# A retention layer in two phases: all projections by seven products first, then the recurrence

## The chip, the cores and the metric

The kernel runs on one core of a Trainium2 chip. The metric is the device time of one execution in microseconds; three runs of the kernel before the change are given, and one more execution was taken by the hardware profiler. In the text PE is TensorE, DVE is VectorE, ACT is ScalarE, POOL is GpSimd and SP is SyncE, whose queue carries most DMAs.

## The reference

Two layers of a hybrid decoder work on 1040 tokens (16 meta tokens and 1024 others) of width 1024, in float32. Layer 0 mixes a gated linear recurrence with windowed attention, layer 1 is a multi-scale retention; each has a SwiGLU feed-forward network behind it. The change lies in the retention:

```python
def _mixer_retention(h, cos, sin, w_in, w_out):
    q, k, v, g = jnp.split(h @ w_in, SPLIT_RET, axis=-1)      # 1024, 1024, 2048, 2048 wide
    q = _rotary(q.reshape(B, T, RET_HEADS, RET_QK_DIM), cos, sin)
    k = _rotary(k.reshape(B, T, RET_HEADS, RET_QK_DIM), cos, sin) * (RET_QK_DIM ** -0.5)
    ...
    def step(state, chunk):                                   # chunks of 128 tokens, 4 heads
        qn, kn, vn = chunk
        qk = jnp.einsum('bhid,bhjd->bhij', qn, kn).astype(F32) * decay_intra
        o = (jnp.einsum('bhij,bhjv->bhiv', qk, vf)
             + jnp.einsum('bhid,bhdv->bhiv', qn.astype(F32) * decay_q[..., None], state))
        state = (decay_chunk[:, None, None] * state
                 + jnp.einsum('bhjd,bhjv->bhdv', kn.astype(F32) * decay_k[..., None], vf))
        return state, o
    ...
    o = _rms_noaffine(o).reshape(B, T, 2 * D_MODEL).astype(h.dtype)
    return (jax.nn.silu(g) * o) @ w_out
```

`h` is the RMS-normed residual stream, and the mixer's result is added to it.

## The kernel before

**Precision and products.** Activations stand feature-major: 8 blocks of 128 features by tokens. Every large product is made of three matmuls (`mm3`, L160 to L162): both operands are split into a high part, rounded by ScalarE to the matmul's short format, and a low part, the difference (VectorE or GpSimd); the product of the two low parts is left out. `part` (L111, L113) splits weights, 512 columns at a time, `hilo` (L782, L783) splits moving blocks.

**Strassen.** The feed-forward layers (`ffn`) use a form of Strassen's scheme with seven products in place of eight. A unit is 256 inputs by 256 outputs per pair of blocks. `unit22` loads a unit of weights, makes the sums S1 to S4 on GpSimd (L145 to L151) and splits seven operands. The moving side is a 2 by 2 block matrix as well: two feature blocks by two halves of the tokens, with T1 to T4 made by `mixed` (L777). `seven` runs the products and calls `evac` after each, which adds or copies PSUM into the result. In front of a layer the T blocks are not there yet; `eight` runs its first two units as plain products.

**The order.** The program is written in one stream, and a planner places every instruction on its engine's queue, by the place in the stream and by when its inputs and its memory are free; engines run their queues in order. SBUF has 56 slots of 531 columns (`slot`), PSUM four banks under `ps` and four under `ax`.

**Layer 0's feed-forward** takes 22 tiles of hidden features, in 11 pairs. The hidden blocks go to DRAM, and the down projection takes them back in groups `DGROUPS` (two, three, three and three pairs) with four units of outputs in each. After a unit of the last group, `done0` prepares that block of the residual stream for the retention: a split of `h` times the gain (`xh`, `xl`, L963) of the first half of the tokens, its square, and the sum of the squares on GpSimd.

**Retention** goes over the tokens in two halves (16 + 512 and 512). In each half, for each of the four heads: values are projected by plain products with the tokens as the stationary operand, 256 columns of weights a time (`wrv`), the meta tokens apart in `mm_meta` (L186); keys and queries by `proj` with 264 or 512 columns and rotated (`rotate`); gates by `proj`. The recurrence over blocks of 128 tokens has `first` (scores L1083, transposed keys L1098), `second` (outputs, state update L1127, split of the state by `to_hilo` L294 and L295) and `third` (transposes L1137, gate, split). Gates and the next head's keys are placed between the blocks (`fill`), then `project` adds the output projection into `h` (L1208). All of the projection weights are thus loaded and split once for each half. The norm factor comes from `stats`, once per half, and is applied behind each projection. For the last head of a half, `prefetch` and `project` also prepare the next stage, for the second half the normed blocks of layer 1's feed-forward (`normed` L762, `plain`).

## Time and profile before

| what | us |
|---|---|
| median of three runs (2689.75 to 2698.34) | 2693.39 |
| the profiled execution, its own time | 2692.1 |
| its span, first to last instruction | 2690.0 |
| to 435: input, layer 0's mixer; PE busy | 403.6 of 435 |
| 435 to 860: layer 0's gate and up; PE busy | 421.7 of 425 |
| 860 to 1093: layer 0's down; PE busy | 221.9 of 233 |
| 1093 to 2010: retention; PE busy | 909.5 of 917 |
| from 2010: layer 1's feed-forward; PE busy | 658.0 of 680 |

The stages overlap at their borders; the limits are read from the rows of the windows. In a row of a window come its limits and its length, then for PE, PE's weight loads, DVE, ACT and POOL the busy time and the number of instructions, then the granted clock of TensorE (1.00 is full speed), the busy share of the DMA engines and GB/s. In a row of a group come line, engine, operation, what it writes and reads, the shape and the count, then busy time in us and the mean in ns, then the idle time of the engine ahead of it and what ended it. In a row of the timeline come the start and the duration in us; a row of the chain of waits has the same two and names what the chain ran through.

### The profile page before, as it was taken

Reading aid. Unit: us, or ns where it says so; the run is one execution under the profiler, and the core shown is the slowest. Engines: PE = TensorE matmul, PEld = TensorE weight load, DVE = VectorE, ACT = ScalarE, POOL = GpSimd, SP = SyncE. Lnnn points to the kernel's source line nnn. Section 1 sums busy time; section 2 is a strip of 40 time slices with the busy share of each in tenths; the row PEclk is TensorE's granted clock in tenths of the full one; section 3 lists DMA queues with packets and bytes.
Section 4 is the critical chain, followed back from the end, with each engine's and each line's share of the span. In section 5 each row is a group of like instructions: output and inputs, shape, how many; then the busy total and the mean of one; then the engine's idle time right before and its main releaser. Section 6 shows DMA issues by size and latency. Waiting matters only on the chain.

```text
span 2690.0 us, 42990 instructions
## 1 busy us (share of the span) xinstructions
PE 2614.7 (97%) x16122; PEld 2328.5 (87%) x16122; DVE 1648.6 (61%) x2967; ACT 1130.2 (42%) x2328; POOL 1324.9 (49%) x1234
## 2 busy tenths in 40 slices
PE   8988999999999999999999999999998999998999
PEld 7877989999998999888889898888886788886787
DVE  7977676666666877543534444344387555556875
ACT  4666543333333434343434534334343333334442
POOL 3756233554554877523323243333353555565884
PEclk9999999999999999999999999999998999999999
DMA  4001142223225642222122242222241232226542
GB/s 153 30 26 56 55 170 69 95 103 112 84 104 171 214 141 89 91 71 79 65 85 70 86 135 71 87 79 71 86 141 62 87 114 98 101 92 236 165 151 86
DMA packets 111072, 274.62 MB, mean 102 GB/s; under 512 B 13520, under 2 KB 13776, under 8 KB 110864
## 3 DMA queue, kind: packets, MB, share of 16 engines
q1 hardware_dynamic: 87840, 228.86, 25.3%
q10 hardware_dynamic: 22464, 41.17, 4.1%
q8 instruction: 126, 2.06, 0.3%
q0 software_dynamic: 560, 1.85, 0.2%
q14 instruction: 82, 0.67, 0.1%
HBM read 216.40 MB, written 55.43 MB: 101 GB/s over the span
## 4 chain that ended last, share of the span: by engine, by line
PE 88%; DVE 6%; ACT 3%; issue 1%; POOL 1%; DMA 1%; SPq 0%; ACTq 0%; DVEq 0%; POOLq 0%
PE ps L160 20%; PE ps L161 20%; PE ps L162 20%; PE ax L160 8%; PE ax L161 8%; PE ax L162 8%; DVE lo L113 1%; PE ps L673 1%; POOL ol L783 1%; DVE ol L783 1%; PE ax L1083 1%; DVE xp L762 1%; PE ax L186 1%; DVE T L777 0%; ACT hi L111 0%
## 5 line engine op out<-in xcount | busy, mean ns | idle before, releaser
L160 PE MATMUL ps<-oh,hi 128*128 128x260 f32 (+1 forms) x1584 | 509.0, 324 | 20.0 <-ACT oh L782 11.6
L162 PE MATMUL ps<-oh,lo 128*128 128x260 f32 (+1 forms) x1584 | 508.3, 322 | 8.7 <-DVE lo L113 8.6
L161 PE MATMUL ps<-ol,hi 128*128 128x260 f32 (+1 forms) x1584 | 509.7, 322 | 1.1 <-DVE ol L783 1.1
L111 ACT CAST hi<-raw 128x512 fp32r<-128x512 f32 (+2 forms) x476 | 284.6, 602 | 520.9 <-PE ps L161 343.4
L160 PE MATMUL ax<-oh,hi 128*128 128x260 f32 (+1 forms) x1212 | 388.8, 323 | 1.7 <-ACT hi L111 0.9
L162 PE MATMUL ax<-oh,lo 128*128 128x260 f32 (+1 forms) x1212 | 387.4, 322 | 2.6 <-DVE lo L113 2.6
L161 PE MATMUL ax<-ol,hi 128*128 128x260 f32 (+1 forms) x1212 | 389.8, 322 | 0.0
L113 DVE TENSOR_TENSOR lo<-raw,hi 128x512 fp32r<-128x512 f32 (+2 forms) x348 | 286.9, 827 | 111.4 <-ACT hi L111 102.3
L160 PEld LDWEIGHTS ps<-oh,hi 128*128 128x128 f32 x1584 | 299.7, 190 | 47.5 <-ACT oh L782 14.7
L111 ACT CAST hi<-S 128x512 fp32r<-128x512 f32 (+2 forms) x288 | 161.2, 562 | 425.3 <-PE ps L161 190.7
L113 DVE TENSOR_TENSOR lo<-S,hi 128x512 fp32r<-128x512 f32 (+2 forms) x288 | 252.1, 878 | 139.5 <-ACT hi L111 136.1
L162 PEld LDWEIGHTS ps<-oh,lo 128*128 128x128 f32 x1584 | 300.3, 190 | 34.6 <-DVE lo L113 10.8
L161 PEld LDWEIGHTS ps<-ol,hi 128*128 128x128 f32 x1584 | 300.9, 190 | 25.8 <-DVE ol L783 2.1
L113 POOL TENSOR_TENSOR lo<-raw,hi 128x512 fp32r<-128x512 f32 x128 | 166.0, 1305 | 266.8 <-ACT hi L111 255.4
L160 PE MATMUL ps<-xh,hi 128*128 128x512 f32 (+1 forms) x752 | 277.2, 371 | 8.2 <-ACT hi L111 7.1
L161 PE MATMUL ps<-xl,hi 128*128 128x512 f32 (+1 forms) x752 | 274.7, 366 | 0.6 <-DVE xl L210 0.6
L162 PE MATMUL ps<-xh,lo 128*128 128x512 f32 (+1 forms) x752 | 273.1, 364 | 0.0
L291 POOL TENSOR_TENSOR t<-t,rf 128x520 f32<-128x520 f32 (+1 forms) x148 | 215.0, 1462 | 81.9 <-DVE t L824 31.7
L162 PEld LDWEIGHTS ax<-oh,lo 128*128 128x128 f32 x1212 | 229.4, 189 | 21.6 <-DVE lo L113 3.6
L160 PEld LDWEIGHTS ax<-oh,hi 128*128 128x128 f32 x1212 | 229.9, 190 | 20.8 <-ACT hi L111 1.3
L161 PEld LDWEIGHTS ax<-ol,hi 128*128 128x128 f32 x1212 | 229.9, 190 | 18.4
L783 POOL TENSOR_TENSOR ol<-raw,oh 128x520 fp32r<-128x520 f32 (+1 forms) x140 | 204.6, 1489 | 28.7 <-ACT oh L782 14.7
(325 smaller groups left out, 5720.7 us busy)
## 6 DMA issues: line engine op xcount, KB each, us to landing
raw<-in_wr_dram SPq DMA_DIRECT2D x64, 512.0 KB, 3.2
raw<-in_wgu_dram SPq DMA_DIRECT2D x48, 512.0 KB, 3.3
rb<-in_wgu_dram SPq DMA_DIRECT2D x40, 512.0 KB, 3.2
raw<-hd SPq DMA_DIRECT2D x77, 260.0 KB, 3.4
raw<-hd SPq DMA_DIRECT2D x77, 256.0 KB, 3.1
raw<-in_wrv_dram SPq DMA_DIRECT2D x32, 512.0 KB, 3.2
raw<-in_wro_dram SPq DMA_DIRECT2D x32, 512.0 KB, 3.2
hd<-T ACTq DMA_DIRECT2D x44, 260.0 KB, 2.6
```

The costliest lines, as they stand in the source:

```text
L111: nc.scalar.copy(hi, src)
L113: eng.tensor_tensor(out=lo, in0=src, in1=f32(hi), op=ALU.subtract)
L160: nc.tensor.matmul(ps, ah, bh, start=first and i == 0, stop=False, skip_group_check=more)
L161: nc.tensor.matmul(ps, ah, bl, start=False, stop=False, skip_group_check=more)
L162: nc.tensor.matmul(ps, al, bh, start=False, stop=last and i == n - 1, skip_group_check=more)
L186: nc.tensor.matmul(o, a, b, start=first and i == 0 and j == 0, stop=end and j == 1)
L291: (eng or nc.vector).tensor_tensor(out=out_, in0=a, in1=b, op=ALU.mult)
L673: nc.tensor.matmul(k.po[:n, o:o + 64], sb[:, i * P:(i + 1) * P], vt[:, k.b - len(segs) + 1 + j, g * 64:(g + 1) * 64], start=False, stop=g ...
L762: nc.vector.scalar_tensor_tensor(out=t[:, :n], in0=h[m][hf][:, :n], scalar=par(gname, m), in1=sc, op0=ALU.mult, op1=ALU.mult)
L783: eng.tensor_tensor(out=lo, in0=src, in1=f32(hi), op=ALU.subtract)
L1083: nc.tensor.matmul(ps[:, :P], kf[d][:, c:c + P], qf[d][:, c:c + P], start=d == 0, stop=d == 1)
```

## The change

The retention is taken apart into two phases.

**Phase one** makes all of the projections, for all tokens and heads, and writes them to DRAM (`kdr`, `qdr`, `gdr`, `vdr`). Its moving side `xo2` has the form of the feed-forward's: normed blocks, both halves of 520 tokens, with T blocks. Two gate units are run by `eight`, the 22 others (four of keys, four of queries, eight of values, six of gates) by `seven`. Keys, gates and values are scaled by the norm factor behind the product; keys and queries are rotated; values, which now come out feature-major, are transposed by TensorE. The weights `wr` hold all four parts in units of the Strassen form, and `wrv` goes.

**Phase two** runs the recurrence head by head over all nine blocks, reading keys, queries, values and gates back from DRAM. Beside each step stands at most one unit of the output projection of the half before (`fills`), none at steps 32 and 33. The last gate unit is placed behind the first step's loads.

**Around it.** `done0` makes normed blocks for both halves (`normed`, `spill`, `plain`) in place of the scaled splits; `late0` computes the product of the norm factors that it needs. `DGROUPS` becomes `DG`, with groups of two, three, two, two and two pairs in layer 0 and the old groups in layer 1. `eight` evacuates each product one product later. In `mixes` the low part of T3 goes to GpSimd. `ratio` can take a slot. `mm_meta` and `stats` are no longer used in the retention.

```diff
-DGROUPS = ((0, 1), (2, 3, 4), (5, 6, 7), (8, 9, 10))
+DG = (((0, 1), (2, 3, 4), (5, 6), (7, 8), (9, 10)), ((0, 1), (2, 3, 4), (5, 6, 7), (8, 9, 10)))
...
     def eight(u, xs, chunks, evac):
+        last = None
         for m, c in ((1, 1), (2, 1), (1, 2), (2, 2)):
...
-            evac(m, c, [ps[:, :b - a] for ps, (a, b) in zip(bk, chunks)])
+            if last:
+                evac(*last)
+            last = (m, c, [ps[:, :b - a] for ps, (a, b) in zip(bk, chunks)])
+        evac(*last)
...
-                    xs[j][k] = hilo(m_[k], n, new(j), nc.vector)
+                    xs[j][k] = hilo(m_[k], n, new(j), nc.gpsimd if k == "T3" else nc.vector)
...
     def done0(m):
-        spill(m, 1, 8, 512)
...
-            nc.scalar.activation(xh[:, o], src, AF.Copy, scale=g)
-            nc.vector.scalar_tensor_tensor(out=xl[:, o], in0=src, scalar=g, in1=f32(xh[:, o]), op0=ALU.mult,
-                                           op1=ALU.subtract)
...
+        for hf in range(2):
+            if m == 0:
+                acc2[hf] = slot("acc")
+            xp[m][hf] = normed(m, hf, "g2", 520, tr[hf], acc2[hf])
+            spill(m, hf, 8, 512)
+            plain(xo2, xp, m, hf, 520, slot, nc.vector)
+
+    ffn(fp, wgu0, wd0, DG[0], xo, Rf, 520, late, done0)
...
+    ALL, REST = ((0, 260), (260, 520)), ((8, 520),)
...
+        def proj7(i, chunks, fin):
+            t = {}
+            def evac(k, bk):
+                if k == 1:
+                    later()
+                key = {0: "11", 1: "11", 2: "12", 3: "22", 4: "22", 5: "12", 6: "21"}[k]
+                if k in (0, 2, 3):
+                    t[key] = slot("t")
+                    each(chunks, lambda o, ps: nc.scalar.copy(o, ps), t[key], bk)
+                    return
+                if k < 6:
+                    each(chunks, lambda o, ps, x: nc.vector.tensor_tensor(out=o, in0=ps, in1=x, op=ALU.add),
+                         t[key], bk, t[key])
+                fin(int(key[0]) - 1, int(key[1]) - 1, t.get(key), bk)
+            seven(unit22(wr[i], 512, ap), xo2, chunks, evac)
...
+        def gate(i):
+            def fin(r, c, t, bk):
+                t = scaled(REST, c, t, bk)[:, 8:520]
+                nc.scalar.activation(t, t, AF.Silu)
+                nc.scalar.dma_start(gdr[2 * i + r][c], t)
+            return fin
...
+                mul(p, a, cR)
+                mul(a, a, sR, nc.gpsimd)
+                nc.vector.tensor_tensor(out=p, in0=p, in1=r_, op=ALU.subtract)
+                nc.gpsimd.tensor_tensor(out=u, in0=u, in1=a, op=ALU.add)
+                nc.scalar.dma_start(dst[0][c], p)
+                nc.scalar.dma_start(dst[1][c], u)
...
+        first8(0, (0, 1))
...
+        first8(1, (2, 3))
+        for hd in range(NH):
+            proj7(4 + hd, ALL, rotary(kdr[hd], ALL))
+            proj7(hd, REST, rotary(qdr[hd], REST))
+        for i in range(8):
+            proj7(16 + i, ALL, valued(i))
+        for i in range(2, 7):
+            proj7(8 + i, REST, gate(i))
...
+        ahead(0)
+        proj7(15, REST, gate(7))
...
+        for i, (k, b) in enumerate(seq):
+            if b < 8:
+                updates(k, b)
+            ahead(i + 1)
+            if b:
+                outputs(k, b)
+            if b < 8:
+                state(k, b)
+            if i and seq[i - 1][1]:
+                third(*seq[i - 1])
+                if seq[i - 1][1] in (4, 8):
+                    k_, hf = seq[i - 1][0], seq[i - 1][1] // 8
+                    fills += [(lambda k_=k_, hf=hf, u_=u_: output(k_.hd, hf, u_, *k_.ys[hf])) for u_ in range(4)]
...
+            if fills and i not in (32, 33):
+                fills.pop(0)()
+        fills.pop(0)()
+        third(*seq[-1])
+        while fills:
+            fills.pop(0)()
+        fills += [(lambda u_=u_: output(NH - 1, 1, u_, *heads[-1].ys[1])) for u_ in range(4)]
+        fills.pop(0)()
+        Rf = [ratio(acc3[0], 512, tr[0][:, 8:520], None)[:, :512]]
```

`ahead(i)` loads a step's blocks from DRAM and runs `first`; `updates` makes the state's increments, `state` adds them and splits the state, `output` is one unit of the output projection, and at the last head it also prepares the blocks of layer 1's feed-forward.

More of the change, by code (lines that the diff above doesn't have):

```diff
@@ L883, in residual @@
                     h[m][hf] = unspill(m, hf, n, xslot if hf and m >= 4 else None)
-        for gi, grp in enumerate(DGROUPS):
+        for gi, grp in enumerate(groups):
             xs = [{} for _ in grp]
@@ L949, in tile_hybrid, with products, late0 @@
         plain(xo, xp, m, 1, 520, fslot, nc.vector)
-    late = (lambda: ratio(acc[1], 520, sc[1], fp), mixes(xo, xp, 520, lambda j: fslot if j == 3 else slot))
-    xn2 = [[None, None] for _ in range(KD)]
+    tr = []
+    def products(R, sc):
+        for r, f in zip(R, sc):
+            tr.append(sl.tile([P, W], F32, tag="R", bufs=3, name=nm("R"))[:, :520])
+            mul(tr[-1], r, f, nc.gpsimd)
+    def late0():
+        r = ratio(acc[1], 520, sc[1], fp)
+        products((Rf[0], r), sc)
+        return r
@@ L952, in tile_hybrid @@
+    late = (late0, mixes(xo, xp, 520, lambda j: fslot if j == 3 else slot))
+    xp = [[None, None] for _ in range(KD)]
+    xo2 = [{} for _ in range(4)]
     acc2 = [None, None]
     def done0(m):
[L955 to L968 removed]
@@ new lines, in tile_hybrid, with rslot, output @@
+        fills = []
+        def rslot(s, dt=F32):
+            return rp.tile([P, 512], dt, tag="xs", bufs=8, name=nm(s))
+        def output(hd, hf, u_, yh, yl):
+            u = unit(wro[hd, u_], eng=nc.gpsimd if u_ % 2 else nc.vector)
+            for j in range(2):
+                m = 2 * u_ + j
+                ps = bank("ps")
+                mm3(ps, [(wterm(u, e, j * P, P, 256), (yh[:, e, :], yl[:, e, :])) for e in range(4)])
+                t_ = h[m][hf][:, :512]
+                nc.vector.tensor_tensor(out=t_, in0=ps, in1=t_, op=ALU.add)
+                if hd == NH - 1:
+                    if m == 0:
+                        acc3[hf] = slot("acc")
+                    xp[m][hf] = normed(m, hf, "g3", 512, tr[hf][:, 8:520], acc3[hf])
+                    spill(m, hf, 0, 512)
+                    plain(xo, xp, m, hf, 512, slot, nc.vector)
@@ L1306, in gu, with down @@
         return ac(pairs(w).reshape(-1, 2, P, 1024))
-    def down(w):
+    def down(w, groups):
         p = pairs(w)
-        return [ac(p[:, :, :, :, g[0]:g[-1] + 1].reshape(4, 2, P, -1)) for g in DGROUPS]
+        return [ac(p[:, :, :, :, g[0]:g[-1] + 1].reshape(4, 2, P, -1)) for g in groups]
     def cols(v):
```

488 lines of the change are left out of this document (224 added, 264 removed).

## The prediction

> **What bounds the kernel now.** I read the profile's first page for the shares of the engines and the chain that ended last, then the windows by stage, then the groups of instructions in the stages that the change touches.
>
> ```profile
> span 2690.0 us, 42990 instructions
> PE 2614.7 (97%) x16122; PEld 2328.5 (87%) x16122; DVE 1648.6 (61%) x2967; ACT 1130.2 (42%) x2328; POOL 1324.9 (49%) x1234
> PE 88%; DVE 6%; ACT 3%; issue 1%; POOL 1%; DMA 1%; SPq 0%; ACTq 0%; DVEq 0%; POOLq 0%
> 1093.00:2010.00 917.00, 909.53 (x5294) 793.55 (x5294) 428.03 (x780) 384.91 (x763) 340.90 (x349) 0.99 0.25 87
> ```
>
> TensorE is busy in 97% of the span and makes 88% of the chain; in the retention layer (the window 1093 to 2010) it is busy 909.5 of 917 us. So fewer matmuls are time saved, and whatever leaves TensorE waiting is time lost. A busy row overstates one matmul, since matmuls overlap; their price is the window divided by their number, in stretches where TensorE never rests:
>
> ```profile
> 500.00:850.00 350.00, 350.00 (x2917) 350.00 (x2916) 224.77 (x318) 130.96 (x265) 181.68 (x132) 1.00 0.27 97
> 2100.00:2400.00 300.00, 300.00 (x1296) 243.12 (x1295) 170.83 (x224) 105.70 (x185) 161.30 (x115) 1.00 0.29 104
> 1136.00:1155.00 19.00, 19.00 (x160) 18.72 (x159) 6.01 (x11) 6.73 (x15) 7.09 (x8) 1.00 0.24 84
> ```
>
> The first is Strassen work with 260 columns: 350/2917 = 0.120 us each. The second is the same with 512 columns: 300/1296 = 0.2315 us. The third is the value projection with 256 columns: 19/160 = 0.119 us. By column they differ by under 2%, so cutting a product into 260s costs nothing of note.
>
> **Part 1: TensorE's work.** What goes, from the groups of the window 1120 to 2010 (each has two sisters, L161 and L162, of the same count):
>
> ```profile
> L160 PE MATMUL ps<-xh,hi 128*128 128x512 f32 x448 | 180.1, 402 | 1.1 <-DVE ts L291 1.1
> L160 PE MATMUL ps<-hi,xh 128*128 128x256 f32 x512 | 143.8, 282 | 0.0
> L160 PE MATMUL ps<-yh,hi 128*128 128x512 f32 x192 | 76.3, 398 | 0.0
> L160 PE MATMUL ps<-yh,hi 128*128 128x256 f32 x128 | 34.9, 285 | 1.5 <-ACT yh L1142 1.0 <-DVE h L1208 0.5
> L186 PE MATMUL ax<-hi,meta 128*48 128x256 f32 x64 | 16.5, 287 | 0.0
> 1661.09 1.31 PE ax L1137 x12
> ```
>
> Queries, gates and half of the keys: 1344 x 0.2315 = 311.1 us. The keys' other half, 8 units x 8 x 2 x 3 = 384 with 264 columns: at 0.120 x 264/260 = 0.122, 46.8. Values: 1536 x 0.119 = 182.4; their meta rows, 2 x 64: 15.2. Output projection: 576 x 0.2315 + 384 x 0.119 = 178.9. Together 734.4.
>
> What comes: two plain gate units (`eight`), 192 x 0.2315 = 44.4; four key units of 7 x 4 x 3 x 2 = 168 with 260 columns, 80.6; four query units of 84 with 512, 77.8; eight value units, 161.3; six gate units, 116.7; the output projection, now all 512 wide, 768 x 0.2315 = 177.8. Values come out feature-major and are transposed: 8 x 18 transposes at 1.31/12 = 0.109 us, 15.7. Together 674.3. The recurrence's own matmuls stay. **Saved: 60 us.** The two `stats` give way to two `ratio`s of about as many instructions.
>
> **Part 2: the way into the projections.** Here the cover of TensorE is thin. Today `done0` makes one scaled split per block; afterwards it makes a normed copy, a square and a split for both halves, 16 each, and all T blocks must exist before the first Strassen unit's third product. The last down group also shrinks from three to two pairs (DG[0]), so a call lasts 84 x 0.120 = 10.1 us instead of 15.1, with the same 14 additions and 7 splits on VectorE. The stretch of today that resembles it is the first down group (two pairs, 870 to 912):
>
> ```profile
> 870.00:912.00 42.00, 38.64 (x292) 37.51 (x291) 39.30 (x78) 22.02 (x48) 29.84 (x26) 0.94 0.76 269
> L113 DVE TENSOR_TENSOR lo<-S,hi 128x256 fp32r<-128x256 f32 x12 | 8.6, 730 | 0.2 <-ACT hi L111 0.2
> L783 DVE TENSOR_TENSOR ol<-raw,oh 128x520 fp32r<-128x520 f32 x5 | 5.7, 1130 | 0.5 <-ACT oh L782 0.4
> L783 POOL TENSOR_TENSOR ol<-raw,oh 128x520 fp32r<-128x520 f32 x15 | 20.9, 1411 | 7.4 <-ACT oh L782 6.8 <-DVE ol L783 0.6
> 905.15 0.42 DVE L113 TENSOR_TENSOR lo<-S,hi 128x256 fp32r<-128x256 f32 x1
> 907.41 1.33 DVE L113 TENSOR_TENSOR lo<-rb,hi 128x256 fp32r<-128x256 f32 x1
> 908.66 0.75 DVE L824 TENSOR_TENSOR h<-ax,h 128x260 f32<-128x260 f32 x2
> 1996.34 0.60 DVE lo L113
> L963 DVE SCALAR_TENSOR_TENSOR xl<-h,pkt,xh 128x520 fp32r<-128x520 f32 x8 | 11.0, 1369 | 0.1
> L762 DVE SCALAR_TENSOR_TENSOR xp<-h,pkt,R 128x512 f32<-128x512 f32 x12 | 11.3, 940 | 1.7 <-DMA h<-keep 1.7
> L777 DVE TENSOR_TENSOR T<-xp,xp 128x520 f32<-128x520 f32 x6 | 5.9, 990 | 0.0
> L783 DVE TENSOR_TENSOR ol<-T,oh 128x520 fp32r<-128x520 f32 x16 | 11.6, 763 | 0.0
> L291 DVE TENSOR_TENSOR sg<-ps,R 128x512 f32<-128x512 f32 x32 | 22.1, 692 | 51.9 <-PE ps L162 51.9
> L113 DVE TENSOR_TENSOR lo<-raw,hi 128x512 fp32r<-128x512 f32 x128 | 92.9, 726 | 55.9 <-ACT hi L111 53.3 <-PE ps L161 1.7
> ```
>
> VectorE is busy 39.3 of 42 us there and TensorE misses 3.4. The same split takes 0.42 us or 1.33 us; an addition from PSUM takes 0.75 for two throughout. So an operation on VectorE with two inputs from SBUF is held up while GpSimd (POOL, 1.41 us an instruction) works.
>
> From the start of the last down group to the third product, TensorE has 4 x 10.1 + 44.4 + four products of 2.9 that need no T (two units') = 96 us of work. VectorE has 56 additions at 0.375, 28 splits of 256, 79 two-input operations of 512 or 520 (16 normed, 16 splits, 16 T, 12 T splits, 15 weight splits, 4 in the ratios), 16 evacuations at 0.69 and about 3 us of small ones.
> - Nothing held: 21 + 28 x 0.42 + 79 x 0.60 + 11 + 3 = 94 us, so TensorE need not wait.
> - At the durations shown: 21 + 28 x 0.73 + 16 x 1.15 (between 0.94 and 1.37) + 16 x 1.13 + 16 x 0.99 + 12 x 0.763 + 15 x 0.726 + 4 x 1.0 + 11 + 3 = 131; successive instructions overlap by up to 0.08 us, which takes about 10 off: 121.
> - All 107 held like the split at 907.41, 0.91 more: 94 + 97 = 191.
>
> So TensorE waits X = 0, 25 or 95 us; I take X = **25**, since its rows are those of the same operations. What the stretch costs today goes off:
>
> ```profile
> 1093.00:1126.00 33.00, 29.34 (x199) 26.57 (x199) 21.50 (x41) 12.13 (x29) 24.56 (x33) 0.87 0.35 121
> 1960.00:2100.00 140.00, 127.63 (x629) 105.66 (x629) 110.51 (x151) 56.95 (x100) 66.88 (x46) 0.94 0.28 96
> 860.00:870.00 10.00, 4.51 (x19) 4.28 (x20) 4.34 (x7) 3.28 (x8) 4.05 (x3) 0.59 1.02 361
> ```
>
> 3.7 us idle and 0.13 x 33 = 4.3 of clock, 8 together. After a pause the granted clock falls (0.59 where TensorE was idle for half); I add 5 for it, bounds 0 and 8 (0.06 x 140, the second row). [...]
>
> **Part 3: inside the projections.** VectorE, ScalarE and GpSimd do per unit of some 20 us what they do in the feed-forward layer at 350.00 of 350 us of TensorE. 12 of 56 slots are left beside the 40 of `xo2` and 4 tables, a rotary unit holds 9. I take 0, bounds 0 and 10. Weights are read once instead of once per half, and the DMA share of 1.02 above belongs to a stretch before the layer; the stores sit on ScalarE's queue behind POOL's last addition, and a late one would hold ScalarE's next cast. That is in the 10.
>
> **Part 4: the recurrence without projections beside it.** A step of the recurrence has 15 matmuls of 512 columns (3.5 us), six transposes (0.65) and the scores, some 4.5 us; one output unit beside it is 24 x 0.2315 = 5.6 us.
>
> ```profile
> L1127 DVE SCALAR_TENSOR_TENSOR S<-S,ax 128x512 f32<-128x512 f32 x56 | 37.1, 683 | 19.1 <-PE ax L162 18.8
> L295 DVE TENSOR_TENSOR so<-S,sh 128x512 fp32r<-128x512 f32 x64 | 43.0, 699 | 15.4 <-ACT sh L294 15.4
> L294 ACT CAST sh<-S 128x512 fp32r<-128x512 f32 x64 | 39.5, 623 | 20.4 <-DVE S L1127 14.2 <-PE ax L162 5.3
> ```
>
> The state's chain is 0.68 + 0.68 (two halves) + 0.62 + 0.70 = 2.7 us and lies beside the output unit. Where there is none (steps 0 to 4, 13, 22, 31 to 33) 4.5 us of TensorE face about 5 to 6 us on VectorE and ScalarE. Ten steps at some 0.5 to 1 us, the loads of a head's start and a fall of the clock: **9** us, an estimate, bounds 0 and 86 (32 x 2.7, nothing hidden).
>
> **Part 5: into the last feed-forward layer.** Today 1960 to 2100 loses 12.4 us idle and 8.4 of clock. The same operations remain, with one half's output units beside the last block and the deferred evacuation in `eight`: **-4**, bounds -15 and 10. `late0` adds two POOL products, hidden under the first unit.
>
> **Sum**, against the profiled execution's own 2692.1 us (span 2690.0; the median of the runs, 2693.39, is 1.3 above): 2692.1 - 60 + X + 5 - 8 + 9 - 4 = 2634 + X = **2659 us**.
>
> **The rivals.**
> - *The cover holds*: VectorE is held seldom, X is 0 to 10, 2634 to 2644. For it: POOL works only part of the stretch. Against it: 39.3 of 42 us at a lighter load.
> - *Half of the operations held* (X of 45 to 65): 2679 to 2699. The saved matmuls are paid back by VectorE.
> - *VectorE becomes the bound, slower than before*: in the last down group and the T blocks. From X = 67 on, that is when (67 + 96 - 94)/97 = 71% of the operations are held like the one at 907.41, the kernel is over 2701; all held, 2729. Against it: the mean rows lie nearer to 0.7 than to 1.33. [...]
> - *The recurrence starves*: the state's chain is not hidden, 86 instead of 9: 2736. For it: projections are what fills the gaps today. Against it: an output unit is twice the chain.
> - *The products do not cost what I count*: excluded within 2% by the three windows.
>
> **Chances.** Forecast (2644 to 2679) 0.48; cover holds 0.24; half held 0.14; VectorE bound 0.08; starving 0.06. About 0.3% (8 us) is what a measurement can tell from no change: below 2685 lies 0.48 + 0.24 + a third of 0.14 less some spread, 0.74; within, 0.12; above 2701, 0.14. The range 2628 to 2702 leaves the two slow rivals and a tail below, 0.2.
>
> **What would show it.** Matmul counts as above, PE's busy time lower by some 60; the windows before the first key unit with VectorE near full and TensorE idle some 25 us; the second phase at about 36 steps in 335 us. I am wrong if TensorE idles inside the value or key units (slots), if the granted clock falls repeatedly in the second phase, or if VectorE has room where TensorE waits.

## The result, and the profile after

The changed kernel takes **2718.87 us** (median of four runs, 2714.14 to 2725.89) against 2693.22 for the kernel before in the same job: 1.0096 of its time, interval 1.0068 to 1.0123. It is slower by about 26 us. The forecast was 2659, with a range that ended at 2702: wrong in sign and 60 us too low. The profiled execution took 2718.94 us, its span is 2717.2.

The first page of the changed kernel, the lines that answer to those of before:

```profile
span 2717.2 us, 43283 instructions
PE 2588.8 (95%) x15734; PEld 2287.1 (84%) x15734; DVE 1819.7 (67%) x3130; ACT 1153.4 (42%) x2425; POOL 1491.8 (55%) x1358
PE 78%; DVE 12%; ACT 3%; issue 3%; POOL 2%; DMA 1%; ACTq 0%; SPq 0%; DVEq 0%; POOLq 0%
```

TensorE has fewer matmuls and is busy 26 us less, but its share of the chain falls from 88% to 78%, and VectorE's doubles. To see where, the span is cut at marks that both kernels have: the first addition of layer 0's down projection (the first start in the rows of L824 and L828) and the last addition of the output projection, the recurrence's end (the last start in the rows of L1208 and L1285). Before and after:

```profile
L824 DVE TENSOR_TENSOR h<-ps,h x192: 411/429/693, 873.8 to 2686.2; 128x260 f32<-128x260 f32 x128, 128x512 f32<-128x512 f32 x64
L1208 DVE TENSOR_TENSOR h<-ps,h x80: 407/691/694, 1230.4 to 2006.4; 128x512 f32<-128x512 f32 x48, 128x256 f32<-128x256 f32 x32
```

```profile
L828 DVE TENSOR_TENSOR h<-ps,h x224: 409/420/693, 880.7 to 2713.2; 128x260 f32<-128x260 f32 x80, 128x512 f32<-128x512 f32 x32
L1285 DVE TENSOR_TENSOR h<-ps,h x64: 675/691/694, 1704.9 to 2040.4; 128x512 f32<-128x512 f32 x64
```

Layer 0's down projection begins 6.9 us later, the stretch from there to the recurrence's end takes 1159.7 us instead of 1132.6, the rest 6.8 us less: +27.2 in all, the difference of the two spans. The windows of the changed kernel between such marks (limits and length, then PE's busy time; the number behind the five engines is the granted clock):

```profile
404.90:880.70 475.80, 463.37 (x3800) 461.30 (x3798) 307.76 (x446) 173.70 (x347) 244.40 (x174) 0.98 0.29 104
880.70:1204.00 323.30, 298.04 (x2160) 281.47 (x2161) 278.38 (x523) 136.82 (x283) 206.88 (x176) 0.97 0.40 129
1204.00:1625.00 421.00, 417.49 (x2797) 383.05 (x2796) 241.80 (x321) 147.68 (x291) 241.16 (x189) 1.00 0.31 103
1625.00:1700.00 75.00, 59.74 (x242) 44.88 (x241) 36.04 (x66) 37.35 (x86) 34.98 (x39) 0.89 0.46 161
1700.00:2040.40 340.40, 319.01 (x1445) 253.23 (x1445) 214.05 (x370) 177.90 (x388) 167.30 (x191) 0.97 0.35 119
2040.40:2717.20 676.80, 657.87 (x2801) 526.42 (x2799) 440.44 (x580) 251.13 (x460) 400.45 (x296) 0.99 0.36 121
```

"Loss" in what follows is TensorE's idle time (length less busy) plus what the clock withheld (length times one less the granted clock, summed over windows of 20 us, since two digits are too coarse for long ones).

| stage | before: length, loss | after: length, loss |
|---|---|---|
| to the end of layer 0's mixer | 404.1, 43.6 | 404.9, 43.7 |
| layer 0's gate and up, to the first down addition | 469.7, 14.3 | 475.8, 21.1 |
| down, and the way into the projections (to 1126; to 1204) | 252.2, 14.8 | 323.3, 35.9 |
| projections (after: 1204 to 1625) and recurrence | 880.4, 4.8 | 836.4, 3.5 + 23.9 + 31.8 |
| layer 1's feed-forward | 683.6, 34.2 | 676.8, 26.2 |
| sum | 2690.0, 111.7 | 2717.2, 186.1 |

The loss grew by 74 us, the work shrank by 47. The projections themselves are dense (417.49 of 421 us). The loss lies ahead of them and in the second phase, 23.9 us of it in its first 75.

### The profile page after: what moved, and what is told of

Same layout as the page of the kernel before. It is cut to its first block, busy times and chain, and to the rows that moved or that the text cites. A ratio compares the mean times of both kernels' runs of the same rounds, so it can differ in the third digit from the quotient of the medians.

```text
span 2717.2 us, 43283 instructions
## 1 busy us (share of the span) xinstructions
PE 2588.8 (95%) x15734; PEld 2287.1 (84%) x15734; DVE 1819.7 (67%) x3130; ACT 1153.4 (42%) x2425; POOL 1491.8 (55%) x1358
## 4 chain that ended last, share of the span: by engine, by line
PE 78%; DVE 12%; ACT 3%; issue 3%; POOL 2%; DMA 1%; ACTq 0%; SPq 0%; DVEq 0%; POOLq 0%
PE ps L160 16%; PE ps L162 16%; PE ps L161 16%; PE ax L160 8%; PE ax L161 8%; PE ax L162 8%; DVE lo L113 3%; DVE ol L783 1%; DVE h L828 1%; DVE T L777 1%; PE ps L673 1%; DVE xp L762 1%; POOL ol L783 1%; PE ps L1097 1%; ACT oh L782 1%
## 5 line engine op out<-in xcount | busy, mean ns | idle before, releaser
L160 PE MATMUL ps<-oh,hi 128*128 128x260 f32 (+1 forms) x2160 | 695.2, 324 | 20.9 <-ACT oh L782 10.3
L162 PE MATMUL ps<-oh,lo 128*128 128x260 f32 (+1 forms) x2160 | 691.5, 323 | 12.8 <-DVE lo L113 12.6
L161 PE MATMUL ps<-ol,hi 128*128 128x260 f32 (+1 forms) x2160 | 694.0, 322 | 0.5 <-DVE ol L783 0.5
L160 PE MATMUL ax<-oh,hi 128*128 128x260 f32 (+1 forms) x1652 | 531.1, 324 | 9.5 <-ACT oh L782 3.8
L161 PE MATMUL ax<-ol,hi 128*128 128x260 f32 (+1 forms) x1652 | 532.1, 323 | 5.3 <-DVE ol L783 5.3
L162 PE MATMUL ax<-oh,lo 128*128 128x260 f32 (+1 forms) x1652 | 527.7, 322 | 0.9 <-DVE lo L113 0.9
L161 PEld LDWEIGHTS ax<-ol,hi 128*128 128x128 f32 x1652 | 313.3, 190 | 31.8 <-DVE ol L783 6.8
L145 POOL TENSOR_TENSOR S<-rb 128x512 f32<-128x512 f32 (+2 forms) x98 | 115.8, 1182 | 317.5 <-DVE lo L113 286.8
L783 POOL TENSOR_TENSOR ol<-raw,oh 128x520 fp32r<-128x520 f32 (+1 forms) x140 | 202.2, 1471 | 24.5 <-ACT oh L782 10.3
L151 POOL TENSOR_TENSOR S<-raw,S 128x512 f32<-128x512 f32 (+2 forms) x98 | 130.8, 1335 | 80.2 <-DVE lo L113 77.4
L146 POOL TENSOR_TENSOR S<-S,raw 128x512 f32<-128x512 f32 (+2 forms) x98 | 116.0, 1183 | 83.3 <-issue 49.3
L149 POOL TENSOR_TENSOR S<-raw,rb 128x512 f32<-128x512 f32 (+2 forms) x98 | 122.7, 1252 | 52.0 <-DVE lo L113 52.0
```

The source lines that it names most:

```text
L145: nc.gpsimd.tensor_tensor(out=s1, in0=a21, in1=a22, op=ALU.add)
L146: nc.gpsimd.tensor_tensor(out=s2, in0=s1, in1=a11, op=ALU.subtract)
L149: nc.gpsimd.tensor_tensor(out=s3, in0=a11, in1=a21, op=ALU.subtract)
L151: nc.gpsimd.tensor_tensor(out=s4, in0=a12, in1=s2, op=ALU.subtract)
L160: nc.tensor.matmul(ps, ah, bh, start=first and i == 0, stop=False, skip_group_check=more)
L161: nc.tensor.matmul(ps, ah, bl, start=False, stop=False, skip_group_check=more)
```

## Experiments

Every kernel is the changed one with the edit shown, unless said otherwise. Each result gives the median, its ratio to the kernel before in the same job, and the 95% interval of the ratio in brackets. Gains are counted from the 2718.9 us above; "before" had a median of 2690.1 to 2690.8 us in these jobs instead of 2693.2, and by the ratios most gains are 1 to 3 us smaller. Kernels whose code is the same in a stage show how far one profile can be trusted: the loss of the way in and the projections (from the first down addition to 30 us ahead of the last gate store) is 38.2 to 40.2 us over eleven kernels, that of the recurrence behind it 50.4 to 57.1 over six.

### Layer 0's feed-forward: evacuation at once

```diff
-                eight(unit4(wgu[0]), xs, chunks, gate0)
+                eight(unit4(wgu[0]), xs, chunks, gate0, n != 520)   # False: evac behind each product
```

> Undoes one part: in layer 0's feed-forward alone, eight evacuates each product at once again; all else is the changed kernel (2718.9 us). Theory A (the late evacuation also puts the ratio's small matmuls one product later, and the T blocks queue up behind them on VectorE): the first addition of the down projection goes back from 880.7 us to about 874, and the kernel to about 2712. Rival (the low part of T3 and the two products of norm factors on GpSimd hold VectorE there): it stays at 880 or so, and the kernel at 2719.

2710.9 us, ratio 1.0077 (1.0062 to 1.0092), an interval that overlaps the changed kernel's; the first addition comes at 877.1 us, halfway between the two theories. From the mixer's last addition to the first down addition this kernel and the four others that carry the edit take 471.4 to 472.3 us, thirteen without it 473.0 to 476.0, the kernel before 469.7 and a variant of it (the last but one experiment) 471.5. So the later evacuation costs some 2 us; the rest of the 6 is hardly more than what single profiles differ by.

### The way into the projections: groups, sums, powers, low parts

```diff
-DG = (((0, 1), (2, 3, 4), (5, 6), (7, 8), (9, 10)), ...
+DG = (((0, 1), (2, 3, 4), (5, 6, 7), (8, 9, 10)), ...
```

> Undoes one part: layer 0's down projection in the four groups of before (two, three, three, three pairs). Theory C (two-pair groups give VectorE 14 additions per 10 us and it cannot keep up): the additions of the down projection span about 232 us again in place of 245; as the last group then takes 42 slots instead of 28, the normed blocks come later and the way into the projections costs some of it back: kernel 2706 to 2716. Rival (the groups do not matter, VectorE catches up behind them): the first key unit starts as late as now, 2719.

2725.2 us, 1.0125 (1.011 to 1.014): nothing won, if anything lost. Layer 0's additions end earlier (1113.9 us instead of 1125.6), but the last gate store comes at 1656.0 as without the edit (1655.8): VectorE's work seems only to be met later.

What the ratio waits for at the entry, GpSimd's timeline of the changed kernel and VectorE's next row:

```profile
1143.25 1.29 POOL L145 TENSOR_TENSOR S<-rb 128x512 f32<-128x512 f32 x1 [4.41 <-DMA rb<-in_wr_dram]
...
1147.09 1.26 POOL L151 TENSOR_TENSOR S<-raw,S 128x512 f32<-128x512 f32 x1
1148.31 1.57 POOL L200 TENSOR_TENSOR rr<-rr,mhalf 128x4 f32<-128x4 f32 x2
```

```profile
1142.37 0.21 DVE L278 TENSOR_SCALAR rr<-ax 128x4 f32<-128x4 f32 x2
1142.60 0.69 DVE L113 TENSOR_TENSOR lo<-raw,hi 128x512 fp32r<-128x512 f32 x1
1149.37 0.87 DVE L284 TENSOR_SCALAR dg<-ckt,rr 128x128 f32<-128x128 f32 x4 [6.08 <-POOL rr L200]
```

The powers (`rr`, L200) could start at 1142.6. On GpSimd's queue four sums for a key unit that is needed much later stand ahead of them, the first after 4.41 us of waiting for its load, and the powers start behind the last one, at 1148.31. VectorE, busy 37.7 of the 40 us from 1100 to 1140, then rests 6.08 us, and TensorE waits 3.40 us of them for `dg` (L285). A first edit took the high priority from these sums:

> The four sums that form the first key unit of phase one (S, on GpSimd, L145 to L151) lose their high priority, so that GpSimd no longer runs them (1143 to 1148.4 in the changed kernel's trace, behind a load of 3.6 us) ahead of the ratio's powers (1148.4 and 1162.1), for which TensorE stands still (6.1 us). Theory A (GpSimd's order is what makes the entry into the projections late): the powers come 5 to 9 us earlier, the loss in the stretch 1080 to 1204 falls from 26.6 us to 17 to 21, the time by 5 to 9 us. Rival (VectorE, busy 39.2 of 40 us in front of it, is the bound; GpSimd's sums only fill its wait): the powers move by under 2 us and the time by under 2 us.

2720.1 us, 1.0104 (1.0087 to 1.0122). GpSimd's order of instructions is the same as before the edit, so this run tells nothing of the theory. The second edit makes the sums wait for the ratio:

```diff
+            if behind is not None:                       # Rr[0], for the first key unit
+                nc.gpsimd.tensor_copy(s1[:, 0:1], behind[:, 0:1])
             nc.gpsimd.tensor_tensor(out=s1, in0=a21, in1=a22, op=ALU.add)
```

> The four sums of the first key unit wait for the ratio's first half, by a copy of one column in front of them, so that GpSimd's order has the ratio's powers first: the step that the experiment with the sums' priority was to take and did not (GpSimd's order of instructions was the same there). Theory A (order on GpSimd): the first powers come about 5 us earlier, right behind VectorE's scaling of the sums, the loss between 1080 and 1204 falls from 26 to 20 to 22 us, the time by 4 to 7 us. Rival V (VectorE is what is late): the time changes by under 2 us, TensorE waits as long for VectorE's lo or dg a few us later.

2710.0 us, 1.0066 (1.0052 to 1.0081): about 8 us. The powers start at 1135.59, right behind VectorE's row:

```profile
1135.36 0.21 DVE L280 TENSOR_SCALAR rr<-ax 128x4 f32<-128x4 f32 x2
...
1137.00 1.00 DVE L286 TENSOR_SCALAR dg<-ckt,rr 128x128 f32<-128x128 f32 x5
```

The loss of the way in falls from 39.4 to 35.5, and the stage to the same mark from 745.1 to 738.0 us; seven kernels with the same code there, the changed one among them, take 742.5 to 745.1. So theory A holds, with some 5 to 8 us. Next VectorE's load (this kernel leaves the low parts out, and its result is not the layer's):

```diff
-        xs[...] = hilo(xp[m][hf][:, :n], n, new, eng)
+        eng.tensor_tensor(out=lo[:, :8], in0=xp[m][hf][:, :8], in1=f32(hi[:, :8]), op=ALU.subtract)
+        xs[...] = hi, hi                                 # for the projections' inputs
```

> The low parts of the sixteen plain blocks that the projections read (16 subtractions on VectorE, 0.7 to 1.8 us each, between 1075 and 1141) are left out but for 8 columns, and the high part is read in their place: the matmuls are as many as before. It takes about 17 us of work from VectorE in front of the projections. Theory V (VectorE is full there and holds the entry): the last addition comes 3 to 5 us earlier, the sums of the ratio 8 to 12 us, the loss between 1080 and 1204 falls from 26 to 14 to 19 us, the time by 7 to 12 us. Rival A (GpSimd waits for the first key unit's load with the powers behind it): the powers stay within 2 us of where they are, the time falls by under 3 us.

2700.6 us, 1.0034 (1.0021 to 1.0048), 18 us less. The stage itself got 11.5 us shorter (733.6 us, loss 33.3); the rest came behind it, 4.5 of it in the last feed-forward, where the instructions are the same, and its cause isn't settled. A kernel that takes work off VectorE and leaves nothing out:

```diff
-        nc.vector.scalar_tensor_tensor(out=t, in0=h, scalar=par(gname, m), in1=sc, op0=ALU.mult, op1=ALU.mult)
+        nc.scalar.activation(t, h, AF.Copy, scale=par(gname, m))      # g2 and g3; the ratio is then the whole norm
```

> The blocks of the projections' and of the last feed-forward's inputs (xp) are made of h and the gain alone, by ScalarE, instead of by VectorE with the earlier norm's factor (16 + 16 operations of 0.74 to 1.9 us); the ratio becomes the whole norm and one VectorE operation shorter. The matmuls are as many. Theory V (VectorE is full at the way into the projections and again at the way into the last feed-forward): the loss between 1080 and 1204 falls from 26 to 12 to 16 us as in the experiment without low parts, the last feed-forward begins 3 to 8 us earlier after the recurrence's last addition, the time falls by 14 to 22 us, to 2696 to 2704 us. Rival (the 17 us fewer were the low parts' alone, since each low part waits for ScalarE's copy in between, and ScalarE is now asked for one more operation of 0.6 us per block): 0 to 5 us.

2695.9 us, 1.0018 (1.0006 to 1.003): 23 us, a little more than theory V had. The loss of the way in is 27.3 instead of 39.4, the stage 729.6 us. How the edit divides between the two entries is shown below, for the mended kernel.

### The start of the recurrence: room for the first values

The chain of waits of the changed kernel, start and duration:

```profile
1657.38 0.49 SPq L1234
1657.91 5.39 DMA h<-keep
1663.32 4.80 DMA vr<-vd
1668.14 0.63 ACT vh L1162
```

The third block's values stand on SP's queue behind loads of gates (L1234) and seven of the residual stream's. The first idea was that these loads are the cause:

```diff
-            if i == 4:                       # 16 loads at once
+            if 4 <= i < 12:                  # two a step, behind a copy of the state's first column
```

> One part alone: the sixteen loads of the residual stream are spread over steps 4 to 11, two a step, each held behind the state by a one-column copy on GpSimd (16 small instructions more). Theory B (at the start of the second phase some 4 MB of loads stand ahead of the value loads on SyncE's queue, and TensorE waits for values): the loss between 1625 and 1700 us, 15 us idle and 8 of clock, falls by 10 to 20, and the kernel goes to about 2704. Rival (the state's chain is what TensorE waits for): no change beyond 3 us.

2713.6 us, 1.0087 (1.0072 to 1.0102), perhaps 2 to 5 us; between 1625 and 1700 TensorE is busy 61.3 us instead of 59.7, and the wait for `kd` (L1195, behind the values) is 12.0 instead of 12.5. So the loads of `h` alone are not what ends the waits. The values' own loads go out late, since their slots belong to the projections' inputs until the last gate unit is through. In the next kernels they land in the buffers of the weight loads:

```diff
-            raw = slot("vr")[:, :512]
+            raw = (raw_tile() if k.hd == 0 and b < 4 else slot("vr"))[:, :512]
```

> Only the first half of the edit before: the first four value loads of head 0 land in the weight loads' buffers, the reloads of h stay together in front of step 4's loads. If the room that the projections' inputs held is the cause, nearly all of the 16 us (2718 to 2702) comes back by this alone: 2702 to 2708 us, and TensorE's waits on kd fall from 13.1 us to under 8 between 1625 and 1995. Rival (the reloads on SP's queue are as much to blame once the loads go out in time): 2710 to 2716 us, and a wait of 4 to 6 us stays at step 4 or 5.

2709.4 us, 1.0066 (1.0051 to 1.0081); the waits on `kd` between 1615 and 1700 fall from 12.5 to 6.7 us. The time lies between the two forecasts. With the spread loads as well:

> The first four value loads of head 0 land in the two buffers of the weight loads instead of in slots that the projections' inputs still hold, and the reloads of h are spread as in the reload experiment (which alone brought about 3 us, with 21.9 us still lost between 1625 and 1700). Theory S (the first steps start late since their values can be loaded only once the last projection is through): the loads go out before the last gate unit, TensorE's waits of 2.6 and 3.1 us at 1635 and 1655 go with the halved clock behind them, the loss in that stretch falls to 10 to 14 us, the time to 8 to 12 us below the changed kernel's. Rival F (the first four steps have no output unit beside them, so each step's own chain sets their time): the loss stays at 20 us or more and the time within 2 us of the reload experiment's, that is 3 to 7 us below the changed kernel's.

2702.3 us, 1.0042 (1.0028 to 1.0055): 16 us, more than either theory had. The stretch from 1625 to 1700 in this kernel (0.89 and 59.74 in the changed one):

```profile
1625.00:1700.00 75.00, 62.07 (x277) 47.52 (x277) 39.62 (x73) 39.76 (x93) 39.57 (x51) 0.98 0.44 148
```

It is mostly the clock that comes back: TensorE still idles 12.9 us there instead of 15.3, but the clock withholds some 2 us instead of some 8. (The last gate store lies 10.7 us earlier in this kernel; the window moved by as much shows nearly the same, 0.98 and 61.55.) Room for the values alone brings 9 us, and the spreading then 7 more, where alone it brought 2 to 5.

### Inside the recurrence: state, banks, order, units

```diff
-            k.sp[d] = (sh, so)               # outputs read the state just split
+            k.sp[d], k.spn[d] = k.spn.get(d, (sh, so)), (sh, so)   # ... the one split a step earlier
```

> The outputs of a block read the split state of one block earlier (the newest block's part of the state is left out of them), so the wait of the outputs for the state's update and split is gone and all the work is still done. Theory B (value loads, head starts, steps without an output unit) expects at most 5 us: 2714 to 2719. Rival, the recurrence starving on the state's chain: the loss of some 42 us between 1625 and 1995 falls by half or more, kernel below 2698.

2718.1 us, 1.01 (1.0084 to 1.0117), and TensorE is busy 281.4 of the 295 us between 1700 and 1995, as without the edit (282.5): the time does not hang on the outputs' wait for the state. (This kernel leaves the newest block's part of the state out of the outputs.) My rival of 2736 us named the wrong chain.

> The transposed outputs (third) take their PSUM bank from the other four, beside the output products and the units. Between the steps the first four banks are wanted by five tiles (two of first, two updates, third), and TensorE waits 4.8 us for yt to free one. Theory B (banks): these waits go, the loss between 1700 and 1995 falls by 3 to 5 us, the time by 2 to 5 us. Rival (the same step waits then for the kd or yh chain instead): under 1.5 us.

(`bank()` becomes `bank("ps")` in `third`.) 2715.5 us, 1.0096 (1.0074 to 1.0119). The 4.8 us of waits on `yt` go, and those on `yh` rise from 3.8 to 12.8 us between 1625 and 1995: the rival. Then the order in a step:

```diff
+            if fills and i not in (32, 33):
+                fills.pop(0)()
             if i and seq[i - 1][1]:
                 third(*seq[i - 1])
...
-            if fills and i not in (32, 33):
-                fills.pop(0)()
```

> Each step's output unit is put ahead of the step's transposes (third) and taken from the list before the step adds its own, so that no unit reads the yh that the same step has just made. Theory H (the dips where a half of a head ends: TensorE waits for yh at L1248, 10.5 us in 5 times with 6.8 of them at the end of the recurrence, and loses the clock): the loss between 1700 and 1995 falls from 18.4 to 11 to 13 us and the time by 5 to 7 us. Rival (the steps are short of work as a whole; the unit-free step only moves from the fourth of a head to the fifth): the dips move, the time changes by under 2 us.

2705.8 us, 1.0053 (1.0035 to 1.0072): 13 us, twice what theory H had. TensorE's waits on `yh` and `yt` (L1248, L1191) are gone from the list between 1700 and 1995, and the waits on `kd` there rise from 0.6 to 7.1 us. The profile places only some 5 us of the 13 in the recurrence (from the last gate store 380.0 us instead of 384.6), which would be theory H's size; the rest lies, 2 to 4 us each, in stages with unchanged code and isn't explained. The longest wait on `yh`, 6.75 us at the recurrence's end, stays (7.04): it has another cause, shown below. Last, the price of a step without a unit, by making twelve more:

```diff
-            if fills and i not in (32, 33):
+            for _ in range((2 if i > 4 and i % 9 in (5, 6, 0, 1) else 0) if i < 32 else int(i > 33)):
```

> The same output units stand two in a step and none in the next two, in the first three heads and the first half of what follows: 12 more steps without a unit, nothing else changed. Theory F (a step without a unit beside it is bound by its own chain over ScalarE, VectorE and GpSimd, and costs TensorE 2 to 5 us with the halved clock behind it): the stretch from the first unit to the end of the recurrence gets 24 to 50 us longer. Rival S (only the loads at the start were late; steps run as well without a unit): under 8 us.

2732.4 us, 1.0154 (1.0139 to 1.0169): 14 us more. From the last gate store to the recurrence's end, the changed kernel and this one, with the same instructions:

```profile
1655.80:2040.40 384.60, 351.73 (x1582) 278.05 (x1583) 240.37 (x424) 204.19 (x452) 191.90 (x221) 0.96 0.38 129
```

```profile
1652.00:2058.50 406.50, 361.77 (x1582) 279.64 (x1583) 243.33 (x424) 202.97 (x452) 194.49 (x221) 0.95 0.37 122
```

21.9 us for 12 steps, 1.8 each in the stretch (1.1 by the medians). Less than theory F, more than S: a step without a unit does cost time. That the doubled units ahead let the other engines run on, and so keep the price down, is a guess.

### Together, and the kernel before with one of the edits

> Four edits in one: the first values in their own room, the reloads of h spread, the output unit one step later, and the gate product of the first feed-forward unit evacuated at once. If their gains add, 16 us, 13 us and about 3 us come off 2718: 2684 to 2690 us, just ahead of the kernel before (ratio 0.998 to 1.000). Rival (the values and the later unit mend the same stretch of the recurrence): 2693 to 2700 us.

2696.6 us, 1.0021 (1.001 to 1.0031): 22 us, within the rival's range: the gains don't add. With the powers first:

> The three-together kernel (2696.6 us) and the ratio's powers ahead of the first key unit's sums (8 us by itself): 2687 to 2692 us if the two stretches are independent, as they lie 450 us apart; 2694 to 2698 us if what is won at the entry is lost again at the start of the recurrence.

2692.9 us, 1.001 (1.0001 to 1.002): 4 us more, half of what it brought alone. With the blocks on ScalarE:

> The kernel before this one in the list with the blocks made on ScalarE as well. If VectorE's load at the two entries is a cost of its own: 2670 to 2680 us, ahead of the kernel before (ratio 0.992 to 0.996). If powers first and the lighter VectorE mend the same wait: 2683 to 2690 us, level with the kernel before.

2678.3 us, 0.9962 (0.9948 to 0.9976): ahead of the kernel before by 12 us. But one part of its edits has nothing to do with the two phases. The kernel before makes the high part for its projections from `h` and the gain on ScalarE already, without an earlier norm, and makes only the last feed-forward's blocks on VectorE. It got that edit alone:

> The kernel before, with the sixteen blocks of the last feed-forward's inputs made on ScalarE from h and the gain, as in the kernel with all mended (its projections' inputs are made on ScalarE already: the kernel before splits h times the gain, without an earlier norm). Where VectorE is busy 43.9 of 50 us and 12.1 of 15 us ahead of that stage it frees about 10 us of it. If that entry is bound by VectorE in this kernel too: 2682 to 2687 us, and the lead of the two phases, all mended (12 us), shrinks to 4 to 9 us. Rival (there the end of the recurrence hides it): within 3 us of 2690, and the lead stands.

**2674.7 us, 0.9939 (0.9925 to 0.9954)**, 16 us, more than either forecast had, and the fastest of all. From the recurrence's last addition on, 98.4 us of the kernel before and of this one:

```profile
2006.40:2104.80 98.40, 88.66 (x359) 69.97 (x359) 72.76 (x94) 34.95 (x62) 46.13 (x31) 0.91 0.22 79
```

```profile
2001.60:2100.00 98.40, 95.21 (x416) 75.41 (x415) 71.73 (x98) 40.34 (x72) 48.01 (x34) 1.00 0.27 92
```

9.7 us of idle time become 3.2, and the clock is full. And the mended kernel with only the projections' inputs on ScalarE:

> All mended, but with the last feed-forward's blocks on VectorE again: only the projections' inputs are made on ScalarE. From 2678.3 us. If the projections' entry has nearly all of the gain that came with this edit (15 us from 2692.9 to 2678.3; the loss between 1080 and 1204 fell from 27 to about 14): 2679 to 2683 us. Rival (the last feed-forward's entry has half of it): 2684 to 2688 us.

2692.1 us, 1.0 (0.999 to 1.001), as without (2692.9). The rival and more: all 14 us of that edit are the last feed-forward's. At the projections' entry it does shorten its stage (727.5 us against 734.1, loss 29.0 against 33.2), yet in that one profile the recurrence behind lost 46.5 instead of 39.6. TensorE idles as long there as before (30.9 and 31.2 us); the difference is clock, and why it was withheld longer isn't settled.

Most of the 14 us lie ahead of the recurrence's last addition, as the traces show. The end of the recurrence in the changed kernel:

```profile
1998.64 0.66 PE L1244 MATMUL ax<-ckt,on 128*128 128x128 f32 x4 [0.53 <-ACT on L1209]
...
2004.32 1.75 DVE L762 SCALAR_TENSOR_TENSOR xp<-h,pkt,R 128x512 f32<-128x512 f32 x1
2005.99 0.68 DVE L1285 TENSOR_TENSOR h<-ps,h 128x512 f32<-128x512 f32 x1
2006.75 0.69 DVE L783 TENSOR_TENSOR ol<-xp,oh 128x512 fp32r<-128x512 f32 x1
2007.36 0.68 DVE L291 TENSOR_TENSOR yt<-ax,sg 128x512 f32<-128x512 f32 x1
...
2008.85 1.65 PE L160 MATMUL ps<-yh,hi 128*128 128x512 f32 x3 [6.75 <-ACT yh L1248]
```

The last block's outputs are transposed by 1999.3, but their product with the gates, `yt`, stands on VectorE's queue behind normed blocks and low parts of the last feed-forward (L762, L783) until 2007.36. TensorE waits 6.75 us; the window from 2000 to 2020 loses 8.3 us of idle time and 5.2 of clock. With the blocks still on VectorE the wait is 7.18 us in the last kernel above; in the one with all mended it is 2.67, and the 40 us ahead of the last addition lose 4.5 us instead of 13.5.

## Why the prediction was wrong

By its own terms, in the loss table's measure:

| term | forecast | measured |
|---|---|---|
| matmuls saved | -60 | -47 |
| into the projections (X + 5 - 8) | +22 | +21 |
| inside the projections | 0 | +3.5 |
| recurrence without projections | +9 | +51 |
| into the last feed-forward | -4 | -8 |
| layer 0's gate and up | not in the sum | +7 |
| sum | -33 | +27 |

- **The products** cost what was counted, though the three prices differ by up to 2.6% per column, not by under 2% as said; the sum takes each by itself, so nothing hangs on it. The key units' stores in the changed kernel:

```profile
L1072 ACTq DMA_DIRECT2D kd<-ro x8: 326/326/327, 1216.9 to 1338.8; - x8
```

Less one product (2.9 us) these are three spacings of a key and a query unit, 39.7 us each; the sum had 20.15 + 19.45 = 39.6. That the table has 47 instead of 60 is mostly the measure: a matmul behind a pause is booked with 0.40 us where the pace is 0.23, and the timeline has 58 pauses between 1080 and 2127 against 16 between 1080 and 2100 before. That hides an estimated 42 x 0.17 = 7 us of loss in the busy time; the other 6 I can't place.
- **The way in** came out at its size, with a mechanism that was only half right. VectorE was nearly full as forecast (37.7 of the 40 us from 1100 to 1140), and taking work off it shortens the stage by 9 to 15 us (no low parts, ScalarE). But 5 to 8 us were GpSimd's order, which the prediction didn't look at, so the agreement of the sizes is partly luck: it priced GpSimd as what holds VectorE up, not as a queue in which the ratio's powers stand behind a load. (That VectorE is held up stands in the trace of before: with GpSimd at rest from 898.84 to 902.28 the splits of 256 columns at 899.71, 901.05 and 901.72 take 0.41 us each; the one at 907.41, beside GpSimd's subtraction at 907.15, takes 1.33.) Moved instructions change what is queued behind what, and of the new key unit's sums I counted nothing. The 5 us for the clock were a choice between bounds; in the changed kernel the clock withheld 8.8 us between 1080 and 1204, beside 17.9 of idle time.
- **Part 4 is the step that failed**: it put the recurrence without projections at 9 us, and the row measured 51, 42 of the 60 us. Some 11 of these belong to the last feed-forward (13.5 us at 2000 to 2020, where the kernel before loses 2.6 in the 46 us ahead of its own mark), so that some 31 are the recurrence's own. The step priced the second phase at ten steps of 0.5 to 1 us, reasoning from the state's chain, 2.7 us, beside an output unit of 5.6. The bound that it kept, 86, was the same chain's. The outputs' wait for that chain costs nothing (the state one behind). What costs: the first steps' values, whose slots the projections' inputs hold (9 us, 16 with the reloads spread); units placed so that they read the `yh` just made (13 by the medians, 5 by the trace); and steps without a unit at 1.1 to 1.8 us each rather than 0.5 to 1. Of these the room was in the prediction's reach: Part 3 counted 12 of 56 slots left and asked only whether a rotary unit fits, not what the first loads of the next phase land in. With all mended the recurrence still loses 31 us where the old order, with projections between the blocks, lost 5 in the whole layer. Ten steps without a unit are 11 to 18 of the 31, an estimate from the prices above. The longest waits left are those on `kd`, 16.3 us in 13 times; no experiment took them away, and their share stays open.
- **The last feed-forward** came out at -8 against -4 by the marks, but with the 13.5 us that its blocks cost ahead of the mark nothing was won: the 140 us from 1994 lose 22.0 us where the 140 from 1960 lost 20.8 before. That "the same operations remain" was right, and they were the largest prize of this case: 14 to 16 us in either kernel.
- **Layer 0's gate and up** wasn't in the sum; the edit to `eight` was read and not priced. It explains some 2 of the 7 us; most of the rest is within what single profiles differ by.
- **The rivals.** "The cover holds" and "VectorE becomes the bound" both took the entry for the deciding place. The rival that chose the right place, the starving recurrence at 0.06, chose the wrong chain. Of the three signs of being wrong under "What would show it" two came true: the clock fell again and again in the second phase (0.89 and 0.97 in its two windows above, 1.00 in the projections), and VectorE had room where TensorE waited (6.08 us at the entry).

The two phases save some 60 us of products and give up the filler that kept TensorE busy between the blocks. Mended, they reach 2678.3 us (0.9962, 0.9948 to 0.9976); the kernel before with the one edit that both can take reaches 2674.7 (0.9939, 0.9925 to 0.9954). So even mended they are no faster here, and the two intervals overlap a little.

## What to carry to other kernels

Work that fills another stage's gaps is worth its own time and the gaps': before moving it away, price the stage that stays behind without it, step by step, and by its worst waits rather than by one chain. A wait at a stage's end can belong to the next stage's work, when that stands ahead on an engine's queue. When a stage begins as another ends, ask what its first loads land in and what stands ahead of them on each queue. And when several edits win, give the old kernel those that it can take before crediting the change.

## What the runs showed of the hardware

A pause of 2.57 us was followed by half the clock. TensorE's timeline of the changed kernel at the first step (start, duration; the starts give the pace):

```profile
1637.49 0.79 PE L160 MATMUL ax<-vh,kd 16*128 16x512 f32 x1 [2.57 <-ACT kd L1195]
...
1640.93 0.63 PE L162 MATMUL ps<-oh,lo 128*128 128x512 f32 x1
1641.36 0.63 PE L160 MATMUL ps<-oh,hi 128*128 128x512 f32 x1
...
1646.99 0.39 PE L162 MATMUL ps<-oh,lo 128*128 128x512 f32 x1
1647.22 0.40 PE L160 MATMUL ps<-oh,hi 128*128 128x512 f32 x1
```

Behind the pause the matmuls start every 0.43 us until about 1644, then every 0.23; the granted clock is 0.50 from 1637.4 to 1644 and 0.98 from there to 1650. So the pause of 2.57 us was followed by about 3.3 us more of loss (6.6 us at 0.50). The other waits of the changed kernel between 1080 and 2127, with the granted clock in the 3 us behind each: the six others of over 2.5 us (2.71 to 6.75 us) 0.50 to 0.71; one of 2.33 us, at 1197.59, and one of 1.79, at 1789.08, 1.00; one of 1.42, at 1739.26, 0.60. The runs don't show what decides between them. In the sum the clock is 26.0 us of the 79.7 us lost between layer 0's last addition and the recurrence's end (20 us windows) and idle time 53.7, so on average a microsecond of waiting there came with about half a microsecond of clock.
